# A planner's key that prefers settled operands, stores on ScalarE's queue, and another end of the last tile

## The chip, the core and the metric

The kernel runs on one core of one Trainium2 chip. The core has TensorE (PE in the profile), VectorE (DVE), ScalarE (ACT), GpSimd (POOL) and SyncE (SP); each executes its own list of instructions in a fixed order and waits at an instruction until what it depends on is done. SyncE only starts DMA transfers; ScalarE and GpSimd can start them too. The metric is the device time of one execution in microseconds; before and after the change it is the median of several executions.

## What is computed

One pre-norm residual block over x of 512 tokens by 1024 channels, in float32:

```
h = rmsnorm(x, norm_g)
q_lat, c_kv, k_rope, z_a, q_b, k_b, v_b, z_b, q_idx, k_idx, w_idx, gate_a, gate_b = split(h @ w_in)
y_a = mla_attention(...)  * silu(z_a)     # 8 heads, low-rank q and kv, rotary key, chunk-causal
y_b = dsa_attention(...)  * silu(z_b)     # 8 heads, an indexer keeps the top 128 keys of each query, relative-position bias
merged = sigmoid(gate_a) * (y_a @ w_o_a) + sigmoid(gate_b) * (y_b @ w_o_b)
out = rmsnorm(x + merged @ w_out, final_g)
```

## The kernel before

**Arithmetic.** Each float32 operand of a matmul is split in two parts, a rounded one (made by ScalarE, a copy at L302) and the rest (a subtraction by VectorE at L328 or GpSimd at L330), and each product is three matmuls (`mm3`, L405, issued at L400: high by high, high by low, low by high). So every weight tile goes through a load (SyncE, L427), a copy (ScalarE), a subtraction (VectorE or GpSimd) and only then the matmuls. Transposes are matmuls against an identity (L417). Scaling rows by a factor is VectorE at L358, GpSimd at L361 or ScalarE at L311; the power of -0.5 of a norm is GpSimd at L378; three-operand steps are VectorE at L339; reductions of scores are L1474 (branch A) and L1571 (branch B).

**Stages.** At the start x and the first weights come in; the indexer, key and latent projections run on unnormalised x, and the factor rstd of the first norm comes in later: four transposes (L417, tile rstd) bring it into a bank, ScalarE copies it to s_rbc, and VectorE uses s_rbc to make the normed input s_h. Then the gate, attention and latent projections follow as jobs in a written order, in which the matmuls of s_h by weight tiles fill TensorE while VectorE and ScalarE work on the heads of branch A (softmax, transposes of the probabilities s_p, products with values vv), then on the heads of branch B. A table of relative biases (bias_table, L835; two matmuls at L852) goes through a DRAM scratch. Eight gate tiles of branch A (w_ga, 128x512 each, tanh of the projection, tile s_sig) do not stay on chip: `gate` (L1170) stores each in that scratch, and `fetch_gates` (L1195) brings them back after the projections. Then both branches' output projections are merged, and the last product by w_out is made of seven block products (in the order 1, 7, 2, 6, 5, 4, 3) whose weight sums are made on chip by `out_job` (L1708 and following; the sums for products 6 and 4 come from the tiles of product 7).

**The order of the work.** The kernel's parts are Python generators that hand steps to a planner (`Flow`, L134 to L242). It holds a time for each engine, for the port that VectorE and GpSimd share and for the DMA, and costs for each step. In each round it takes, over all parts, the step with the smallest key (L204): the planned start, plus 0.01 times the part's priority, plus a small random nudge drawn from a seed (DRAW, L248). Where a step may run on several engines, it takes the one that ends soonest by the plan. The instruction is recorded at once, so the order of planning is the order of each engine's list on the chip. Nothing of the plan's times enters the program, only this order and the choice of engines. A step that is planned late moves all that comes behind it on its engine.

**The end.** The last product's results are read by `finish` (L1760): x is added, the squares are summed (by ScalarE in `square`, L1782, or for the last piece of a token tile by a VectorE reduce at L1768), and the row is multiplied by final_g. `scale_out` (L1786) adds the partial sums of squares with eps (L1790), adds the third one where a tile has three pieces (L1793), takes the power on GpSimd (L1795), scales the left half on VectorE and the right half on ScalarE (L1797), and has SyncE store both (L1800). The token tiles 2 and 3 end earlier, tiles 0 and 1 last.

Of the kernel before, what the change touches and what calls it, by code (L numbers as in the profile page):

```python
# [133 lines left out]
class Flow:  # L134
# [24 lines left out]
    def advance(self, t, value):  # L159
        try:  # L160
# [2 lines left out]
            t.alive = False  # L163
            self.threads.remove(t)

    def start(self, step, eng):
        s = self.free[eng]
        for b in step.ins:
            if not b.written and b not in step.outs:
                return math.inf  # L170
            s = max(s, b.w + (RAW_LAG.get(eng, 0.0) if b.by == eng else self.lat(b.by, eng)))
        for b in step.outs:
            if not eng == b.by == "SP":
                s = max(s, b.w + self.lat(b.by, eng))
            for e, r in b.reads.items():
                s = max(s, r + self.lat(e, eng))
        return max(s, self.port) if self.shares(step, eng) else s
# [5 lines left out]
    def run(self, stop=None):  # L183
        while self.threads:
            if stop and stop():
                return
            moved = False
            for t in sorted(self.threads, key=lambda t: t.prio):
                if isinstance(t.req, Get):
                    b = t.req.pool.give(t.req)  # L190
                    if b is not None:
                        self.advance(t, b)
                        moved = True
                elif isinstance(t.req, Until) and t.req.cond():
                    self.advance(t, None)
                    moved = True
            if moved:
                continue
            best = None
            for t in self.threads:  # L200
                if isinstance(t.req, Step):
                    for i, (eng, dur, emit) in enumerate(t.req.options):
                        s = self.start(t.req, eng)
                        key = (s + BIAS * t.prio + t.nudge, t.prio)  # L204
                        if len(t.req.options) > 1:
                            fin = s + dur + {"POOL": self.pbias if t.req.pbias is None else t.req.pbias, "ACT": t.req.abias}.get(eng, 0.0)
                            cand = (fin, s, eng, dur, emit, key)
                        else:
                            cand = (0.0, s, eng, dur, emit, key)
                        if i == 0 or cand[0] < mine[0]:  # L210
                            mine = cand
                    if best is None or mine[5] < best[1][5]:
                        best = (t, mine)
            if best is None or best[1][1] == math.inf:
                raise RuntimeError("stuck: " + "; ".join(f"{t.gen.__name__}@{t.gen.gi_frame.f_lineno} {type(t.req).__name__} {getattr(t.req, 'cls', '')}" for t in self.threads))
            t, (_, s, eng, dur, emit, _) = best
            emit()
            step = t.req
            if eng == "SP":

                self.free["SP"] = s + 0.05
                self.hw = max(self.hw, s) + (0.65 if step.ins and step.outs else 0.475)
                self.dma = max(self.dma, self.hw + 0.65)

                self.dma += dur * (SLOW if self.dma < 7.3 else 1.0)
                end = self.dma + (2.2 if step.ins and step.outs else 1.0) + step.late
            else:
                self.free[eng] = end = s + dur
                if self.shares(step, eng):
                    self.port = end  # L230
                if step.moves and eng == "ACT":

                    end += 1.8 + step.moves
                elif step.moves:
                    self.dma = max(self.dma, end + 1.0) + step.moves
                    end = self.dma + 1.0
            for b in step.ins:
                b.r = b.reads[eng] = max(b.r, end)
            for b in step.outs:
                b.w = max(b.w, end)  # L240
                b.written, b.by = True, eng
            self.advance(t, None)  # L242
# [2 lines left out]
RAW_LAG = {"DVE": 0.125, "POOL": 0.1, "ACT": 0.1}  # L245
BIAS = 0.01
NUDGE = 0.01
DRAW = 71  # L248
TC_ARGS = {}


# [1 line left out]
def tile_block(ctx: ExitStack, tc: tile.TileContext, a: dict, out: bass.AP, bias_dram: bass.AP):  # L253
# [181 lines left out]
    def act_dma(dst, src):  # L435
        step = Step([("ACT", 0.06, lambda: nc.scalar.dma_start(dst.ap, src))], bufs(dst), [])
        step.moves = 4.0 * dst.n * dst.ap.shape[0] / 360000
        return step

    def backward(v):  # L440
# [729 lines left out]
    def gate(name, c, how=proj):  # L1170


        def take(ps):
            if in_ps(ps.all):
                s = yield slot("sig")
                yield act(s.all.f, ps.all, AF.Tanh, scale=0.5)
                put(ps)
            else:
                s = ps
                yield act(s.all.f, s.all.f, AF.Tanh, scale=0.5)  # L1180
            if c in away and name == "w_ga":
                yield dma(spilt(c), s.all.f)
                put(s)
                done.add(("spilt", c))
            else:
                sig[name, c] = s

        how(name, c, take, 12)
# [3 lines left out]
    def spilt(c):  # L1192
        return bass.AP(bias_dram.tensor, NH * NREL + c * P * S, [[S, P], [1, S]])
# [514 lines left out]
    def out_job(product, c):  # L1708

        h, g = {1: (0, 0), 2: (0, 1), 3: (1, 1), 4: (0, 1), 6: (0, 0)}.get(product, (0, 0))  # L1710

        def prep(job):
            raw = [job.raw[:, 512 * i : 512 * i + 512] for i in range(2)]
            if product in (1, 2, 3):
                for i in range(2):
                    yield from split_b(raw[i], (product, 2 * c + i), i == 1)
            elif product in (5, 7):
                t = yield slot("wsum")
                yield soon(tt(t.all.f, raw[1], raw[0], ALU.subtract, BOTH))
                put(job.raw)  # L1720
                yield from split_b(t.all.f, (product, c), product == 5)
                if product == 7:
                    sums[c] = t
            else:
                for i in range(2):
                    yield Until(lambda: 2 * c + i in sums)
                    t = sums[2 * c + i].all.f
                    yield soon(tt(t, raw[i], t, ALU.add if product == 6 else ALU.subtract, BOTH))
                    if i == 1:
                        put(job.raw)  # L1730
                    yield from split_b(t, (product, 2 * c + i), product == 4)

        if product == 5:
            src = w_pair(w_block(0, 0, c), w_block(1, 0, c))
        elif product == 7:
            src = w_pair(w_block(1, 0, c), w_block(1, 1, c))
        else:
            src = a["w_out"][4 * h + 2 * g + c]
        Job(src, [512, 512], None, prep=prep)
# [20 lines left out]
    def finish(t, half, c0, c1, ps, nth, last, keep=False):  # L1760
# [4 lines left out]
            put(ps)  # L1765
        done.add(("read", t, nth))
        if last:
            step = Step([("DVE", 0.1 + 0.00104 * r.n, lambda: nc.vector.tensor_tensor_reduce(  # L1768
                junk.tile[:, : r.n], r.ap, r.ap, op0=ALU.mult, op1=ALU.add, scale=1.0, scalar=0.0,
                accum_out=ssf[t].tile[:, nth : nth + 1]))], [junk, ssf[t]], bufs(r))  # L1770
            step.count = 2
            yield step
            done.add(("sq", t, nth))
            yield is_done(("sum", t))
        else:
            spawn(square(t, r, nth), 0)
        if (t, half) not in rg:
            rg[t, half] = yield slot("rg")
        yield stt(rg[t, half].all.f[:, c0:c1], r, D ** 0.5, fg[half].all.f[:, c0:c1], ALU.mult, ALU.mult)
        done.add(("g", t, nth))  # L1780

    def square(t, r, nth):  # L1782
        yield act(junk[:, : r.n], r, AF.Square, accum=ssf[t][:, nth : nth + 1])
# [2 lines left out]
    def scale_out(t, count):  # L1786

        rs = yield Get(SMALL)
        yield Until(lambda: ("sq", t, 0) in done and ("sq", t, 1) in done)
        yield ts(rs[:, 0:1], ssf[t][:, 0:1], ssf[t][:, 1:2], D * EPS, ALU.add, ALU.add)  # L1790
        if count == 3:
            yield is_done(("sq", t, 2))
            yield tt(rs[:, 0:1], rs[:, 0:1], ssf[t][:, 2:3], ALU.add)  # L1793
        done.add(("sum", t))
        yield power(rs[:, 0:1])  # L1795
        yield Until(lambda: all(("g", t, i) in done for i in range(count)))
        for half, engs in ((0, ("DVE",)), (1, ("ACT",))):  # L1797
            x = rg[t, half].all.f
            yield scale_by(x, x, rs[:, 0:1], engs)
            yield dma(out[TOK[t], half * 512 : (half + 1) * 512], x)  # L1800

    def product(n, banks, left, cols, more=False):

# [256 lines left out]
```

## Time and profile before

| | |
|---|---|
| median of 3 runs | 426.47 us (426.45, 426.47, 428.28) |
| profiled execution, its own time | 427.16 us |
| its span in the trace | 425.4 us |
| granted clock of TensorE, mean | 0.995 |
| TensorE: matmul, weight loads | 415.3 us (98%), 363.9 us (86%) |
| VectorE, ScalarE, GpSimd | 380.5 us (89%), 262.2 us (62%), 109.5 us (26%) |
| matmuls | 2313 |
| DMA | 65.89 MB, mean 155 GB/s |

A row of a timeline reads: start and length in us, engine, line, operation, what it writes <- what it reads, shapes, and xN for N in a row of the same kind; in brackets the idle time of the engine in front of it and what released it. "SPq" and "ACTq" are the parts of SyncE and ScalarE that start transfers. Matmuls overlap (the next starts before the last has drained), so the length of one is more than its share, and the distance from start to start is the better measure. A row of the waits view gives: engine and line that waited, the engine, tile and line waited for, total us, times, longest.

### The profile page before, as it was taken

The numbers are of one execution on the slowest core, as the hardware profiler recorded it, in microseconds if no ns is written. First come the engines' busy times: TensorE is split into PE (matmuls) and PEld (weight loads), VectorE is DVE, ScalarE is ACT, GpSimd is POOL, SyncE is SP. The second block draws the span as 40 slices with busy tenths as digits, with TensorE's granted clock in tenths as the row PEclk, the third lists the DMA queues.
The fourth block names the chain that finished last, engine by engine and source line by source line (L and its number), as shares of the span: only waits on it lengthen the run. The fifth ranks groups of instructions, "written<-read, shape, count | busy, mean of one in ns | idle before, by whom it ended". The sixth has DMA issues, their size and how long they took to land.

```text
span 425.4 us, 7106 instructions
## 1 busy us (share of the span) xinstructions
PE 415.3 (98%) x2313; PEld 363.9 (86%) x2313; DVE 380.5 (89%) x815; ACT 262.2 (62%) x587; POOL 109.5 (26%) x131
## 2 busy tenths in 40 slices
PE   8999999999999999999999999999999999999993
PEld 6999868889888888888899988998998888888883
DVE  4789899999999999999879888988799757999995
ACT  6778786585573758544864677494598524436624
POOL 1037865455355723121300101000010002210212
PEclk9999999999999999999999999999999999999998
DMA  8973137817255450285243525425523887453705
GB/s 258 394 278 112 52 100 207 230 45 186 82 139 148 127 160 1 79 256 173 63 128 121 171 79 157 146 65 178 146 79 124 266 322 252 143 180 106 242 0 197
DMA packets 30277, 65.89 MB, mean 155 GB/s; under 512 B 4648, under 2 KB 5688, under 8 KB 30240
## 3 DMA queue, kind: packets, MB, share of 16 engines
q1 hardware_dynamic: 29264, 64.08, 48.5%
q0 software_dynamic: 832, 1.22, 0.9%
q8 instruction: 18, 0.29, 0.3%
q14 instruction: 19, 0.16, 0.1%
q10 hardware_dynamic: 144, 0.13, 0.1%
HBM read 50.49 MB, written 4.21 MB: 129 GB/s over the span
## 4 chain that ended last, share of the span: by engine, by line
PE 54%; DVE 30%; DMA 7%; ACT 4%; issue 4%; POOL 0%; POOLq 0%; SPq 0%; DVEq 0%; ACTq 0%
PE ps L400 50%; DVE mask L826 4%; DMA raw<-w_out 4%; DVE sm L825 3%; PE ps L417 2%; DVE sm L1474 2%; DVE s_ph L328 2%; DVE s_mg L328 2%; DVE s_wsum L328 1%; DMA s_sig<-bias_scratch 1%; DVE s_tmp L328 1%; ACT s_p L311 1%; DVE s_pair L328 1%; DVE s_wo L328 1%; DVE s_w L328 1%
## 5 line engine op out<-in xcount | busy, mean ns | idle before, releaser
L400 PE MATMUL ps<-s_h,s_w 128*128 128x512 f32 (+1 forms) x732 | 170.9, 379 | 0.0
L400 PEld LDWEIGHTS ps<-s_h,s_w 128*128 128x128 f32 x732 | 127.8, 189 | 21.8 <-issue 0.3
L302 ACT CAST s_w<-raw 128x512 fp32r<-128x512 f32 (+3 forms) x124 | 71.6, 593 | 17.8 <-DVE raw L328 9.2
L330 POOL TENSOR_TENSOR s_w<-raw,s_w 128x512 fp32r<-128x512 f32 (+2 forms) x35 | 44.7, 1284 | 130.1 <-ACT s_w L302 123.9
L328 DVE TENSOR_TENSOR s_w<-raw,s_w 128x512 fp32r<-128x512 f32 (+2 forms) x89 | 58.7, 670 | 5.3 <-ACT s_w L302 4.7
L400 PE MATMUL ps<-s_ys,s_w 128*128 128x512 f32 x192 | 43.7, 389 | 0.0
L400 PEld LDWEIGHTS ps<-s_ys,s_w 128*128 128x128 f32 x192 | 36.0, 188 | 7.5
L311 ACT ACTIVATE s_p<-s_p,sm 128x384 f32<-128x384 f32 (+3 forms) x54 | 29.2, 559 | 6.8 <-DVE sm L1571 5.6
L400 PE MATMUL ps<-s_wo,s_mg 128*128 128x512 f32 (+1 forms) x156 | 33.0, 373 | 0.0
L400 PE MATMUL ps<-s_w,s_xg 128*128 128x328 f32 (+1 forms) x192 | 32.5, 323 | 0.0
L400 PEld LDWEIGHTS ps<-s_wo,s_mg 128*128 128x128 f32 x156 | 27.6, 188 | 5.2
L400 PEld LDWEIGHTS ps<-s_w,s_xg 128*128 128x128 f32 x192 | 31.4, 188 | 0.0
L328 DVE TENSOR_TENSOR s_ph<-ps,s_ph 128x384 fp32r<-128x384 f32 (+1 forms) x48 | 27.4, 590 | 2.5 <-ACT s_ph L302 2.3
L302 ACT CAST s_ph<-ps 128x384 fp32r<-128x384 f32 (+1 forms) x48 | 23.5, 514 | 5.5 <-PE ps L417 4.2
L311 ACT ACTIVATE s_p<-ps,sm 128x128 f32<-128x128 f32 (+3 forms) x32 | 16.8, 527 | 15.5 <-DVE sm L1474 15.1
L826 DVE MATCH_REPLACE8 mask<-sm,mask 128x384 f32<-128x384 f32 (+2 forms) x48 | 25.8, 540 | 0.0
L825 DVE MAX8 sm<-mask 128x8 f32<-128x384 f32 (+2 forms) x48 | 25.5, 547 | 0.1
L400 PE MATMUL ps<-s_ph,vv 128*128 128x512 f32 (+3 forms) x128 | 24.9, 325 | 0.0
L417 PE MATMUL ps<-ident,s_p 128*128 128x128 f32 x160 | 24.2, 275 | 0.5 <-DVE s_p L358 0.3
L417 PEld LDWEIGHTS ps<-ident,s_p 128*128 128x128 f32 x160 | 18.8, 140 | 4.7 <-ACT s_p L311 1.0
L400 PEld LDWEIGHTS ps<-s_ph,vv 128*128 128x128 f32 x128 | 20.6, 189 | 2.1 <-DVE s_ph L328 0.2
L400 PE MATMUL ps<-s_lat,s_w 128*128 128x512 f32 x78 | 20.5, 398 | 0.0
(197 smaller groups left out, 737.5 us busy)
## 6 DMA issues: line engine op xcount, KB each, us to landing
raw<-w_out SPq DMA_DIRECT2D x18, 512.0 KB, 4.0
s_op<-s_op SPq DMA_DIRECT2D x36, 128.0 KB, 2.3
raw<-w_ga SPq DMA_DIRECT2D x8, 512.0 KB, 4.5
raw<-w_gb SPq DMA_DIRECT2D x8, 512.0 KB, 4.4
raw<-w_o SPq DMA_DIRECT2D x16, 256.0 KB
s_x<-xT SPq DMA_DIRECT2D x8, 256.0 KB, 4.9
s_xn<-x SPq DMA_DIRECT2D x8, 256.0 KB, 5.7
bias_scratch<-s_sig SPq DMA_DIRECT2D x8, 256.0 KB, 2.5
```

The lines of the kernel that those rows point to most:

```text
L302: nc.scalar.copy(dst.ap, src.ap)
L311: nc.scalar.activation(dst.ap, src.ap, func, **kw)
L328: opts.append(("DVE", 0.07 + 0.00104 * x.n, lambda: nc.vector.tensor_tensor(dst.ap, x.ap, y.ap, op=op)))
L330: opts.append(("POOL", 0.15 + 0.0021 * x.n, lambda: nc.gpsimd.tensor_tensor(dst.ap, x.ap, y.ap, op=op)))
L400: nc.tensor.matmul(ps.ap, l.ap, r.ap, start=start and i == 0, stop=stop and i == len(pairs) - 1, skip_group_check=more)
L417: nc.tensor.transpose(d.ap, s.ap, ident.tile)
L825: yield Step([("DVE", t, lambda: nc.vector.max(m8.tile, work.tile))], [m8], [work])
L826: yield Step([("DVE", t, lambda: nc.vector.match_replace(work.tile, m8.tile, work.tile, MARK))], [work], [m8])
L1474: yield Step([("DVE", 0.07 + 0.00104 * n, lambda: nc.vector.tensor_reduce(mx.tile[:, 1:2], ps.tile[:, :n], op=ALU.max, axis=AX.X, negate=T ...
```

## The change

Five things are edited.

1. `settled()` is added to the planner. For steps on PE and on SP the key uses, in place of the planned start, the latest of that start and, for each buffer read or written, the moment another engine last wrote or read it plus 2.0 us (PE, behind VectorE, ScalarE or GpSimd), 1.0 us (PE behind a transfer) or 1.0 us (SP behind one of the three). The start itself stays as planned; only the choice of the next step changes. The seed goes from 71 to 53.
2. The gates' stores are issued by ScalarE's queue (`act_move`).
3. The weight sums of product 4 wait in the plan until product 6's right operand exists.
4. In the tiles 0 and 1 the partial sum (eps and the two first pieces) is handed to the last reduce as its starting value, and the power reads its result; the separate add goes. Tile 0's left half is scaled by ScalarE. The last store (tile 1, right half) is issued by ScalarE's queue.
5. The part `square` gets the priority -50 in place of 0.

```
+    def settled(self, step, eng, start):
+        s = start
+        for b in (*step.ins, *step.outs):
+            for e, t in ((b.by, b.w), *b.reads.items()):
+                if e != eng and e in SETTLE[eng]:
+                    s = max(s, t + self.lat(e, eng) + SETTLE[eng][e])
+        return s
...
-                        key = (s + BIAS * t.prio + t.nudge, t.prio)
+                        key = ((self.settled(t.req, eng, s) if eng in SETTLE and s < math.inf else s) + BIAS * t.prio + t.nudge, t.prio)
...
-DRAW = 71
+DRAW = 53
+PSQUARE = -50
+SETTLE = {'PE': {'DVE': 2.0, 'ACT': 2.0, 'POOL': 2.0, 'SP': 1.0}, 'SP': {'DVE': 1.0, 'ACT': 1.0, 'POOL': 1.0}}
...
+    def act_move(dst, src):
+        d = dst.ap if isinstance(dst, View) else dst
+        step = Step([("ACT", 0.3, lambda: nc.scalar.dma_start(d, src.ap))], bufs(dst), bufs(src))
+        step.moves = 4.0 * src.n * src.ap.shape[0] / 360000
+        return step
...
             if c in away and name == "w_ga":
-                yield dma(spilt(c), s.all.f)
+                yield act_move(spilt(c), s.all.f)
...
-                    yield Until(lambda: 2 * c + i in sums)
+                    yield Until(lambda: 2 * c + i in sums and (product == 6 or (6, 2 * c + i) in right))
...
         if last:
+            yield Until(lambda: t in partial_sum)
+            s = partial_sum[t]
             step = Step([("DVE", 0.1 + 0.00104 * r.n, lambda: nc.vector.tensor_tensor_reduce(
-                junk.tile[:, : r.n], r.ap, r.ap, op0=ALU.mult, op1=ALU.add, scale=1.0, scalar=0.0,
-                accum_out=ssf[t].tile[:, nth : nth + 1]))], [junk, ssf[t]], bufs(r))
+                junk.tile[:, : r.n], r.ap, r.ap, op0=ALU.mult, op1=ALU.add, scale=1.0, scalar=s.tile[:, 0:1],
+                accum_out=s.tile[:, 1:2]))], [junk, s], [r.buf, s])
...
-            spawn(square(t, r, nth), 0)
+            spawn(square(t, r, nth), PSQUARE)
...
+        r = rs[:, 0:1]
         if count == 3:
-            yield is_done(("sq", t, 2))
-            yield tt(rs[:, 0:1], rs[:, 0:1], ssf[t][:, 2:3], ALU.add)
+            if t < 2:
+                partial_sum[t] = rs
+                yield is_done(("sq", t, 2))
+                r = rs[:, 1:2]
+            else:
+                yield is_done(("sq", t, 2))
+                yield tt(r, r, ssf[t][:, 2:3], ALU.add)
         done.add(("sum", t))
-        yield power(rs[:, 0:1])
+        yield power(r)
...
-        for half, engs in ((0, ("DVE",)), (1, ("ACT",))):
+        for half, engs in ((0, ("ACT",) if t == 0 else ("DVE",)), (1, ("ACT",))):
             x = rg[t, half].all.f
-            yield scale_by(x, x, rs[:, 0:1], engs)
-            yield dma(out[TOK[t], half * 512 : (half + 1) * 512], x)
+            yield scale_by(x, x, r, engs)
+            dst = out[TOK[t], half * 512 : (half + 1) * 512]
+            if t == 1 and half:
+                yield Step([("ACT", 0.06, lambda: nc.scalar.dma_start(dst, x.ap))], [], bufs(x))
+            else:
+                yield dma(dst, x)
```

More of the change, by code (lines that the diff above doesn't have):

```diff
@@ L1780, in finish @@
         done.add(("g", t, nth))
+    partial_sum = {}
     def square(t, r, nth):
```

## The prediction

> **What bounds the kernel now.** I read the page's head first: the span, and the busy time of each engine.
>
> ```profile
> span 425.4 us, 7106 instructions
> ...
> PE 415.3 (98%) x2313; PEld 363.9 (86%) x2313; DVE 380.5 (89%) x815; ACT 262.2 (62%) x587; POOL 109.5 (26%) x131
> ```
>
> TensorE (PE) is busy for 415.3 of 425.4 us, so 10.1 us of the span are not matmul. Both kernels hold the same 2313 matmuls, and the change takes none away. What it can win lies in those 10.1 us and in matmuls that start late although the row calls the engine busy. Next I cut the span by stages (columns: length, then busy time of PE, of its weight loads, of VectorE (DVE), ScalarE (ACT) and GpSimd (POOL), clock, DMA share, GB/s).
>
> ```profile
> 45.00:58.00 13.00, 12.03 (x68) 9.67 (x66) 11.06 (x17) 9.69 (x22) 10.86 (x15) 1.00 0.25 72
> 92.00:160.00 68.00, 68.00 (x374) 58.60 (x373) 67.66 (x172) 39.80 (x97) 35.05 (x42) 1.00 0.48 132
> 160.00:212.00 52.00, 51.74 (x258) 43.06 (x257) 49.94 (x109) 32.26 (x75) 13.64 (x12) 1.00 0.40 117
> 416.00:425.40 9.40, 2.57 (x22) 2.37 (x20) 4.98 (x15) 3.85 (x8) 1.69 (x3) 0.79 0.59 223
> ```
>
> Of the 10.1 us, 6.8 (9.40 less 2.57) lie in the end after the last matmul, and the stages between have tenths of a us to 1.0. In 92 to 160 PE has no gap at all, while VectorE works 67.66 of 68 us: there VectorE has no room, but its lateness does not yet reach PE. The view of PE's waits names what is left:
>
> ```profile
> PE ps L498 <- DVE neghalf L454: 1.1, 1, 1.1
> PE ps L852 <- DVE mask L339: 1.0, 1, 1.0
> ```
>
> The first is the start (L498, the warm-up) and stays: the two orders on PE agree for the first 166 instructions, to about 27 us. The second is one matmul at 57.97. The view counts only idle time; a matmul that is issued late also shows in the distance of starts. PE's timeline at three places (start, duration, of so many):
>
> ```profile
> 56.35 0.65 PE L803 MATMUL ps<-s_qs,s_qs 96*128 96x512 f32 x2
> 57.97 0.31 PE L852 MATMUL ps<-s_oh,rbs 64*8 64x320 f32 x1 [0.97 <-DVE mask L339]
> ```
> ```profile
> 165.04 0.94 PE L400 MATMUL ps<-s_h,s_w 128*128 128x512 f32 x3
> 165.82 0.49 PE L417 MATMUL ps<-ident,s_p 128*128 128x128 f32 x3
> 166.07 0.94 PE L400 MATMUL ps<-s_h,s_w 128*128 128x512 f32 x3
> 167.26 0.70 PE L417 MATMUL ps<-ident,s_p 128*128 128x128 f32 x3 [0.26 <-DVE s_p L358]
> ```
> ```profile
> 212.09 0.38 PE L417 MATMUL ps<-ident,s_p 128*128 128x128 f32 x2
> 212.73 0.44 PE L417 MATMUL ps<-ident,s_p 128*128 128x128 f32 x2 [0.25 <-ACT s_p L311]
> ```
>
> Three 128x512 matmuls take 0.78 us from start to start (165.04 to 165.82), 0.26 each; three transposes 0.25 (165.82 to 166.07), 0.083 each. So the matmul at 57.97 was due at 56.35 + 2 x 0.26 = 56.87 and is 1.10 late. That at 167.26 was due at 166.07 + 0.78 = 166.85: 0.41 late, and its group of three takes 0.70 in place of 0.49, 0.21 more. That at 212.73 was due at 212.09 + 2 x 0.083 = 212.26: 0.47 late. Together 2.2 us. This is all that I can find for a better order to win before the end.
>
> **The change part by part.** *The order (settled(), DRAW).* The key now favours, on PE, operands that were finished 2 us ago, so a matmul on a fresh operand is put behind others. I laid the two built orders side by side. Where a short chain of VectorE or ScalarE work springs from one matmul and another waits for its end, I added up the matmul work between them and took the chain's own durations off: less than 2 us is left over at 61 places before and at 12 after, less than 1 us at 14 and at 4. The late matmul at L852 now waits only for a ScalarE copy that starts 22 matmuls earlier. Number of waits: 434 before, 448 after, so waits are moved, not removed. I take the late time in proportion to the tight places: 2.2 x 12/61 = 0.4 stay, **-1.8 us**. Ends: all of it goes, -2.2; none goes, 0 (new waits could cost more: the slower rival).
>
> One place gets tighter. The four transposes of rstd come later:
>
> ```profile
> 25.70 1.20 PE L400 MATMUL ps<-s_xg,s_w 128*128 128x384 f32 x6
> 26.75 0.60 PE L400 MATMUL ps<-s_w,s_xg 128*128 128x328 f32 x3
> 27.19 0.60 PE L417 MATMUL ps<-ident,rstd 128*128 128x128 f32 x4
> ```
> ```profile
> 27.82 0.59 ACT L302 COPY s_rbc<-ps 128x512 f32<-128x512 f32 x1 [1.27 <-PE ps L417]
> ```
>
> Nine more 128x328 matmuls stand ahead of them (9 x 0.147 by 26.75 to 27.19: VectorE's work on the normed input starts up to 1.3 us later), and behind them only three 128x384 matmuls before one that writes the bank that the copy at 27.82 must first have read; before, twelve stood there. From the last transpose's start, 27.19 + 3 x 0.083 = 27.44, to the copy's end at 28.41 are 0.97 us. The last transpose and three matmuls at 0.175 (25.70 to 26.75 for six) cover 0.61: **+0.3 us** (0.36, less an unknown bit since ScalarE may be free sooner). Ends 0 and 0.4, plus 1.3 if VectorE's lateness reached a matmul; I take it as covered, since the next late matmul is 30 us on.
>
> *VectorE and GpSimd.* The planner's choices shift: VectorE 764 to 746 instructions in the built order, ScalarE 503 to 519 (9 of these issue stores), GpSimd 134 to 144. VectorE's relief I cost at nothing: in the stage where it has no room, PE has no gap to give back. GpSimd's extra is a rival's.
>
> *The gates' stores.* Eight 256 KB stores go from SyncE's queue to ScalarE's.
>
> ```profile
> SPq L427 <- ACT s_sig L311: 11.9, 4, 7.5
> ```
> ```profile
> 55.26 0.33 SPq L427 DMA_DIRECT2D bias_scratch<-s_sig  x1
> ```
> ```profile
> 0.73 0.41 ACTq L436 DMA_DIRECT2D s_er<-w_qi  x1
> ```
>
> SyncE's queue stood 11.9 us behind such stores, with weight loads behind them; now these go sooner. ScalarE has just made s_sig itself, so it waits for nobody there and pays the issue: 8 x 0.41 = 3.3 us, against 62% busy. No wait of PE names a DMA, so the loads gain nothing: 0. Ends: -0.5 (loads that let a weight split start sooner) and +3.3 (every issue delays a copy that PE awaits; the nearest row, ScalarE's 39.80 of 68, speaks against it). The Trainium skill, "DMA: Bandwidth & Descriptors", section "Issuing engines are not separate DMA queues", says that starting DMAs from several engines saves only the sequencer's time for starting them, usually small beside the transfer. By it the move is worth 8 x 0.33 = 2.6 us of SyncE, which would change my sum by nothing; the waits row differs, since SyncE was held 11.9 us by stores that were not ready.
>
> *The sums of weights for product 4* wait for product 6's operand: an order on VectorE beside a PE that is 100% busy; 0, ends -0.2 and +0.5 (one VectorE operation late at PE).
>
> *The end.* The tail's rows:
>
> ```profile
> 419.16 0.72 ACT L311 ACTIVATE s_rg<-s_rg,sm 128x512 f32<-128x512 f32 x1 [0.30 <-POOL sm L378]
> 419.36 0.48 DVE L358 TENSOR_SCALAR s_rg<-s_rg,sm 128x512 f32<-128x512 f32 x1
> 419.75 0.42 DVE L1768 CUSTOM_DVE_ANT_0 junk<-s_xr 128x256 f32<-128x256 f32 x1
> 419.86 2.61 SPq L427 DMA_DIRECT2D out<-s_rg  x4
> 420.09 0.08 DVE L1768 DVE_READ_ACCUMULATOR2_ANT ssf<- 128x1 f32 x1
> 420.21 0.16 DVE L328 TENSOR_TENSOR sm<-sm,ssf 128x1 f32<-128x1 f32 x1
> 420.29 0.42 DVE L339 SCALAR_TENSOR_TENSOR s_rg<-s_xr,s_fg 128x256 f32<-128x256 f32 x1
> 420.45 0.66 POOL L378 TENSOR_TENSOR sm<-sm,neghalf 128x1 f32<-128x1 f32 x1 [1.32 <-DVE sm L328]
> 421.15 0.72 ACT L311 ACTIVATE s_rg<-s_rg,sm 128x512 f32<-128x512 f32 x1 [1.27 <-POOL sm L378]
> ```
>
> The scale at 419.36 moves to ScalarE, so the reduce starts at 419.36 and not 419.75 (-0.39); the separate add goes, and GpSimd's power starts 0.2 sooner after the read at 420.09 (0.28 less some 0.08 to hand over). Power begins at about 419.86 and ends at 420.5. But ScalarE now scales three halves: 419.16 + 2 x 0.72 = 420.6, only then the last: 420.6 in place of 421.15, **-0.5**. Its store is issued by ScalarE right behind (421.35 to 421.75), where SyncE's four stores ended at 419.86 + 2.61 = 422.47: up to -0.7. I take -0.5, ends -0.2 (the issue waits for the engine to drain) and -0.7.
>
> **Sum:** -1.8 + 0.3 - 0.5 = -2.0 us. The profiled execution took 427.16 us (span 425.4 and 1.76 around it), so 425.2; it is 0.69 above the median of the runs, 426.47, so on the median **424.5**.
>
> **Rivals.** (a) *The order changes nothing, only the end does*: each wait that goes is replaced by one of the same size (434 waits against 448 speak for it; the counts of tight places against): 426.47 - 0.5 = 426.0. (b) *All gains at their ends*: -2.2 - 0.5 - 0.7 = -3.4, 423.1; for it, the L852 stall alone is half. (c) *GpSimd slows VectorE in front of PE, and it is slower.* The late matmul at 167.26 comes from this:
>
> ```profile
> 165.57 0.96 DVE L358 TENSOR_SCALAR s_p<-s_p,sm 128x512 f32<-128x512 f32 x1
> ```
> ```profile
> 165.14 1.11 POOL L330 TENSOR_TENSOR s_tmp<-s_tmp 128x256 f32<-128x256 f32 x1 [6.08 <-DVE sm L1441]
> ```
>
> The same scale took 0.48 at 419.36, with GpSimd idle; here it took 0.96 beside a GpSimd operation. Ten more GpSimd operations come, and in 92 to 160 VectorE has 0.34 us of room. Price: up to 1.1 us for a stall like that at 57.97. Five of them turn -2.0 into +3.5, 430.0; to be slower than 428.6 it takes four. The filler matmuls left behind the last head of branch A shrink from 60 to 30 (7.8 us at 0.26), which speaks for it; that VectorE loses 18 operations speaks against. The Trainium skill, "GPSIMD Engine Reference", section "1. Specifications", has GpSimd share its SBUF interfaces with VectorE, with contention where VectorE reads two inputs from SBUF or runs in a two-port mode. The rows at 165.57 and 165.14 agree; no run here shows which mode it was. (d) *The change doesn't do what it says*: the late time stays because hardware times differ from the planned ones; it gives (a)'s time.
>
> **How the numbers follow.** About 0.5% (2.1 us: below 424.34 or above 428.60) is what a measurement of this kernel can tell from no change. The forecast case, 423.8 to 425.3, gets 0.45 and straddles 424.34; (b) and near it 0.20; (a) and (d), 425.3 to 427.0, 0.20; (c) 0.15, most of it beyond 428.6. The first gives 0.23 to faster and 0.22 to the same; (b) adds 0.20 to faster; (a) and (d) 0.20 to the same, and (c) 0.02 to the same and 0.13 to slower. Faster 0.43, same 0.44, slower 0.13. The range goes from 423.0 ((b), and the small gains of loads) to 427.3 ((a) with the bank stall and one new late matmul: 426.0 + 0.3 + 1.0).
>
> **What would show it.** Right: no wait of PE at L852 and L417 over 0.2 us, stages 45 to 58 and 160 to 212 with PE fully busy, one gap of 0.3 us near 28.5, the last power starting about 0.5 us behind the reduce's start (0.7 now), the last store issued by ACTq. Wrong: PE waits of over 1 us in sum behind 92 us, above all for L358 or L328 of VectorE with a GpSimd row beside them; a wait of PE for a DMA; ScalarE's copies late behind an ACTq row; or a span whose loss lies in the first 27 us, where I expect no difference.

## The result and the profile after

| | before | changed |
|---|---|---|
| runs beside each other, 20 each: median (lowest to highest) | 428.25 us (426.27 to 429.81) | 425.64 us (425.31 to 427.45) |
| ratio of the two, 95% interval | | 0.9954 (0.9938 to 0.997) |
| profiled execution, span | 427.16, 425.4 us | 425.62, 423.8 us |

The ratio goes by the means of the runs. The change makes the kernel faster by 0.46% (0.30 to 0.62%), 2.0 us on 426.47. The two profiled executions differ by 1.54 us, the two lowest runs by 0.96. In the profiles of three kernels below (the order alone, the additions late, the seed 12) the matmuls at about 7 us run slower, which costs some 1.6 us (last section); how many of the timed runs began so is not known, so I compare profiles by places behind 10 us.

The page of the changed kernel, its head:

```profile
span 423.8 us, 7086 instructions
...
PE 414.7 (98%) x2313; PEld 364.3 (86%) x2313; DVE 368.9 (87%) x797; ACT 265.1 (63%) x594; POOL 132.3 (31%) x141
```

VectorE is busy 11.6 us less, GpSimd 22.8 us more, TensorE as before. The stages that the prediction showed, and two more (same columns):

```profile
45.00:58.00 13.00, 13.00 (x71) 10.77 (x70) 10.01 (x16) 10.56 (x23) 11.49 (x14) 1.00 0.33 99
58.00:92.00 34.00, 34.00 (x172) 29.05 (x172) 23.98 (x47) 23.30 (x57) 18.26 (x19) 1.00 0.57 160
92.00:160.00 68.00, 68.00 (x376) 58.83 (x375) 65.91 (x178) 42.15 (x102) 36.68 (x45) 1.00 0.48 132
160.00:212.00 52.00, 52.00 (x270) 44.43 (x269) 51.60 (x116) 31.15 (x70) 24.30 (x25) 1.00 0.41 120
212.00:260.00 48.00, 47.19 (x334) 43.90 (x334) 42.40 (x90) 32.56 (x73) 2.75 (x2) 1.00 0.38 124
415.00:423.80 8.80, 2.43 (x21) 2.23 (x19) 4.06 (x12) 4.40 (x9) 1.33 (x2) 0.84 0.63 238
```

TensorE has no gap left from 45 to 58 (0.97 us before) and from 160 to 212 (0.26). But from 212 to 260 it now idles 0.81 us; the same row of before shows 0.25:

```profile
212.00:260.00 48.00, 47.75 (x353) 45.15 (x352) 40.58 (x84) 31.56 (x68) 1.36 (x1) 1.00 0.40 125
```

TensorE's waits after the change. The wait at the bias table and those at the transposes are gone; two waits for steps on s_pair (0.6 us for VectorE, 0.2 for ScalarE) and one for the copy s_rbc are new:

```profile
PE ps L516 <- DVE neghalf L472: 1.1, 1, 1.1
PE ps L411 <- DVE s_pair L339: 0.6, 1, 0.6
PE ps L411 <- ACT s_xg L322: 0.5, 1, 0.5
PE ps L411 <- DVE s_xg L350: 0.2, 1, 0.2
PE ps L411 <- ACT s_pair L313: 0.2, 1, 0.2
PE ps L411 <- ACT s_rbc L313: 0.2, 1, 0.2
```

The bank of the rstd copy, in the changed kernel's PE timeline:

```profile
25.49 1.20 PE L411 MATMUL ps<-s_xg,s_w 128*128 128x384 f32 x6
...
28.31 0.60 PE L428 MATMUL ps<-ident,rstd 128*128 128x128 f32 x4
28.67 0.77 PE L411 MATMUL ps<-s_w,s_xg 128*128 128x384 f32 x3
29.59 0.62 PE L411 MATMUL ps<-s_w,s_xg 128*128 128x384 f32 x2 [0.16 <-ACT s_rbc L313]
```

Three 128x384 matmuls last 0.52 us from start to start; the next began 0.92 behind the first, so 0.40 late: the new stall that the prediction named. The six matmuls at 25.49 stood at 25.70 before: 0.21 us of lead comes from the start, where the order is the same.

Where TensorE stands ahead can be read from groups that both kernels have. First the group of 48 matmuls, and what follows; before:

```profile
220.19 5.92 PE L400 MATMUL ps<-s_w,s_hs 128*128 128x256 f32 x48
225.95 3.04 PE L400 MATMUL ps<-s_w,s_h 128*128 128x256 f32 x24
```

and after:

```profile
217.86 5.92 PE L411 MATMUL ps<-s_w,s_hs 128*128 128x256 f32 x48
223.62 3.04 PE L411 MATMUL ps<-s_w,s_h 128*128 128x256 f32 x24
227.23 2.03 PE L411 MATMUL ps<-s_w,s_hs 128*128 128x256 f32 x15 [0.57 <-DVE s_pair L339]
```

At the 48 matmuls, and at the 24 behind them, the changed kernel is 2.33 us ahead; then a matmul waits. The last product's 36 matmuls show what is left; before, then after:

```profile
412.77 5.80 PE L400 MATMUL ps<-s_wo,qhi 128*128 128x512 f32 x36
```
```profile
411.63 5.80 PE L411 MATMUL ps<-s_wo,qhi 128*128 128x512 f32 x36
```

1.14 us ahead: half of the gain was given back between 223 and 412. The end behind this point (span less 412.77 and 411.63) takes 12.6 us before and 12.2 after.

What gives it back? VectorE's row at the wait, and SyncE's loads, in the changed kernel:

```profile
225.79 0.69 DVE L339 TENSOR_TENSOR s_wsum<-raw 128x512 f32<-128x512 f32 x1 [0.91 <-DMA raw<-w_gb]
226.40 0.68 DVE L339 TENSOR_TENSOR s_pair<-ps,s_pair 128x512 f32<-128x512 f32 x1
```
```profile
219.28 2.17 SPq L438 DMA_DIRECT2D raw<-w_gb  x2
```

and in the kernel before:

```profile
225.38 0.68 DVE L328 TENSOR_TENSOR s_wsum<-raw 128x512 f32<-128x512 f32 x1
...
226.70 0.68 DVE L328 TENSOR_TENSOR s_pair<-ps,s_pair 128x512 f32<-128x512 f32 x1
```
```profile
219.43 1.58 SPq L427 DMA_DIRECT2D raw<-w_gb  x2
```

The step on s_wsum needs the second of the two loads of w_gb, and the read of the bank (s_pair) stands behind it in VectorE's list. Both loads wait for a raw buffer that a VectorE step frees. The first starts at 219.28 (219.43 before), and the issue of the second ends at 221.45 (219.28 + 2.17) where it ended at 221.01 (219.43 + 1.58) before. So VectorE, busy 51.60 of the 52 us up to 212, had gained nothing: the read of the bank starts at 226.40 in place of 226.70, 0.3 us earlier, while TensorE came 2.33 earlier. At 0.12 us for a matmul (48 in 5.76, 220.19 to 225.95) the 24 at 223.62 are through by 226.50, so the next, at 227.23, is 0.73 late. A second matmul is 0.39 late, behind a copy by ScalarE (231.62 + 12 x 0.12 = 233.06 was due):

```profile
231.62 1.60 PE L411 MATMUL ps<-s_hs,s_w 128*128 128x256 f32 x12
233.45 1.70 PE L411 MATMUL ps<-s_h,s_w 128*128 128x256 f32 x12 [0.23 <-ACT s_pair L313]
```

These two places make up the 1.2 us. In short, TensorE ran 2.3 us ahead of a supply that had hardly moved, and met it. This is read from one trace of each kernel; no run below changes these waits alone.

### The profile page after: what moved, and what is told of

The parts are those of the page before. It is cut to its first block, busy times and chain, and to the rows that moved or that the text cites. A ratio compares the mean times of both kernels' runs of the same rounds, so it can differ in the third digit from the quotient of the medians.

```text
span 423.8 us, 7086 instructions
## 1 busy us (share of the span) xinstructions
PE 414.7 (98%) x2313; PEld 364.3 (86%) x2313; DVE 368.9 (87%) x797; ACT 265.1 (63%) x594; POOL 132.3 (31%) x141
## 4 chain that ended last, share of the span: by engine, by line
PE 91%; DVE 3%; DMA 2%; ACT 2%; issue 1%; POOL 0%; POOLq 0%; DVEq 0%; ACTq 0%; SPq 0%
PE ps L411 81%; PE ps L428 5%; PE ps L1510 1%; PE ps L1511 1%; PE ps L1509 1%; DMA raw<-w_gb 1%; PE ps L821 1%; DVE s_w L339 1%; DMA s_er<-w_qi 1%; ACT s_w L313 1%; DVE raw L339 1%; DVE s_xr L350 1%; POOL sm L389 0%; DVE s_pair L339 0%; ACT s_p L322 0%
## 5 line engine op out<-in xcount | busy, mean ns | idle before, releaser
L341 POOL TENSOR_TENSOR s_w<-raw,s_w 128x512 fp32r<-128x512 f32 (+2 forms) x43 | 55.4, 1296 | 56.2 <-ACT s_w L313 39.0
L339 DVE TENSOR_TENSOR s_w<-raw,s_w 128x512 fp32r<-128x512 f32 (+2 forms) x81 | 52.5, 664 | 3.5 <-ACT s_w L313 3.0
L322 ACT ACTIVATE s_p<-s_p,sm 128x128 f32<-128x128 f32 (+3 forms) x60 | 31.2, 550 | 5.3 <-DVE sm L1589 4.9
L341 POOL TENSOR_TENSOR s_pair<-s_pair 128x256 f32<-128x256 f32 x2 | 2.2, 1108 | 99.1 <-DVE s_pair L339 97.8
L844 DVE MATCH_REPLACE8 mask<-sm,mask 128x256 f32<-128x256 f32 (+2 forms) x48 | 25.8, 541 | 0.0
L843 DVE MAX8 sm<-mask 128x8 f32<-128x256 f32 (+2 forms) x48 | 25.4, 548 | 0.3
L313 ACT COPY s_tmp<-ps 64x512 f32<-64x512 f32 (+1 forms) x18 | 10.1, 563 | 19.2 <-PE ps L411 19.2
```

The lines of the kernel that those rows point to most:

```text
L313: nc.scalar.copy(dst.ap, src.ap)
L322: nc.scalar.activation(dst.ap, src.ap, func, **kw)
L339: opts.append(("DVE", 0.07 + 0.00104 * x.n, lambda: nc.vector.tensor_tensor(dst.ap, x.ap, y.ap, op=op)))
L341: opts.append(("POOL", 0.15 + 0.0021 * x.n, lambda: nc.gpsimd.tensor_tensor(dst.ap, x.ap, y.ap, op=op)))
L843: yield Step([("DVE", t, lambda: nc.vector.max(m8.tile, work.tile))], [m8], [work])
L844: yield Step([("DVE", t, lambda: nc.vector.match_replace(work.tile, m8.tile, work.tile, MARK))], [work], [m8])
```

## The experiments

All ratios are to the kernel before, on the same chip. The waits and stages are from the profile of each run.

**The end alone.** The edits of the end put into the kernel before; TensorE's built order is that of before. Diff: points 4 and 5 of the change.

> The kernel before with the end's edits alone (partial sum into the last reduce, tile 0's left half on ScalarE, last store by ScalarE's queue, priority of the squares); TensorE's built order is that of before, instruction by instruction. My theory (order and end both pay): the last power starts about 0.5 us behind the reduce's start, the end after the last matmul's start is 0.4 us shorter (7.10 before, 6.70 in the changed kernel), and the time falls by 0.3 to 0.5 us, ratio near 0.999. Rival (the order changes nothing, only the end does): the whole difference of the changed kernel, ratio near 0.9954. TensorE's late waits stay: 1.1 us at the second matmul of the bias table, 0.4 and 0.5 at the transposes.

Measured: 0.9993 (0.997 to 1.0015). The wait at the bias table stays. In its profile the last power starts 0.57 us behind the reduce's start (419.46 and 418.89), and the end behind the start of the last 36 matmuls takes 12.0 us (412.42 of 424.4) in place of 12.6. In the time the end by itself is worth too little for this measurement, as expected of a few tenths.

**The order alone.** Diff to before: point 1 of the change (`settled()`, SETTLE, `DRAW = 53`).

> The kernel before with the planner's settled key and the seed 53 alone; gates' stores on SyncE's queue, the end as before. My theory: TensorE's late time falls by about 1.1 to 1.8 us (the three late matmuls go, the stall of 0.3 us at the bank of the rstd copy comes), ratio 0.996 to 0.9975. Rival (only the end pays): ratio 1.000 within 0.001.

Measured: 0.9959 (0.9938 to 0.998). So the order carries the change; the rival that only the end pays falls. In its profile the six 128x384 matmuls that start at 25.70 before start at 27.06, 1.36 later, and the last 36 matmuls at 413.06, only 0.29 later: between these two places the order won 1.07 us. In the changed kernel it won 0.93 between them (0.21 ahead, then 1.14).

**The gates' stores back on SyncE.**

```
-                yield act_move(spilt(c), s.all.f)
+                yield dma(spilt(c), s.all.f)
```

> The changed kernel with the gates' eight stores back on SyncE's queue; 70 of TensorE's 2328 instructions stand elsewhere. My theory (the stores' queue is worth nothing): within 0.3 us of the changed kernel. Rival (SyncE held up by stores that are not ready makes weight loads late): 1 us or more slower than the changed kernel, with waits of TensorE behind weight splits; a second rival (ScalarE's eight issues of 0.34 to 0.41 us are on the path): 0.5 us or more faster.

Measured: 0.9956 (0.9938 to 0.9974), profiled execution 425.56 us (changed kernel: 425.62). The store queue is worth nothing that shows, in either direction. Point 3 of the change and the squares' priority leave the built order as it is, instruction by instruction, when each is taken out, so they have no effect here.

**The last store back on SyncE.**

```
-            if t == 1 and half:
+            if False:
```

> The changed kernel with the very last store back on SyncE's queue; all other instructions are the same. In the changed kernel ScalarE's issue at 419.98 lands at 422.745, 2.76 us later, where SyncE's last store of before took 2.26. Theory A (ScalarE's queue starts a transfer later than SyncE's): by SyncE the store is issued at 420.12 and lands at 422.3 to 422.4, the time falls by 0.3 to 0.4 us. Theory B (the landing is set by three stores of 256 KB that come within 0.8 us of each other): it lands at 422.75 to 422.9, the time is the same or 0.15 us longer.

Measured: 0.9945 (0.9921 to 0.9968), profiled execution 425.60 us. The time from issue to landing of the stores of `out` (least, median, greatest of the three whose landing the trace has), in the changed kernel and here:

```profile
DMA to landing us min/median/max: 2.0/2.3/2.8
```
```profile
DMA to landing us min/median/max: 2.0/2.3/2.6
```

SyncE issues 0.23 us later (420.22 in place of 419.98) and its store takes 2.6 in place of 2.8 us: it lands at the same time, about 422.8. That fits theory B, that three stores of 256 KB close to each other set the landing and not the queue.

**The seed alone, and the key alone.** Before with `DRAW = 53`; before with `settled()` and SETTLE at seed 71.

> The kernel before with the seed 53 in place of 71 and nothing else: its built order has 29 places with less than 1 us and 62 with less than 2 us of matmul work in hand (before: 14 and 61). Theory A (the settled key makes the gain, the seed is chance): late time of TensorE as in before or above, 2 us and more behind 27 us, time 0 to 2 us above before. Theory B (the seed was the gain): time 0.7 to 2 us below before.

> The kernel before with the settled key at the old seed 71: 5 places under 1 us and 12 under 2 us, as few as in the changed kernel (4 and 12). Theory A (the key makes the gain): TensorE's late time falls below 1.5 us, no wait at the bias table, time near that of the order alone with seed 53 (0.7 to 2 us below before). Theory B (the seed): time within 0.5 us of before.

Measured: seed alone 1.0242 (1.0205 to 1.028), key alone 1.0218 (1.0179 to 1.0257). Both theories of both runs fall: neither part makes the gain, each alone costs 9 to 10 us. TensorE's late time on short chains did fall with the key alone (no wait at the bias table), but it meets this, in the last stage:

```profile
408.44 6.02 POOL L340 TENSOR_TENSOR s_wo<-s_wsum,s_wo 128x512 fp32r<-128x512 f32 x1
...
409.64 3.68 DVE L338 TENSOR_TENSOR s_xr<-s_xr,s_part 128x512 f32<-128x512 f32 x6
...
415.79 0.67 DVE L338 TENSOR_TENSOR s_wo<-s_wsum,s_wo 128x512 fp32r<-128x512 f32 x1
416.52 0.74 PE L410 MATMUL ps<-s_wo,s_mg 128*128 128x512 f32 x2 [3.65 <-DVE s_wo L338]
```

VectorE's list has six additions of s_xr, and more work for the end, in front of the weight split that the next matmuls need. With the seed alone the same wait is 6.5 us. The built orders show it before any run: a split of s_wo behind the additions in these two and in the next kernel, none in the kernel before and the changed one. A planner that takes what can start first puts the additions in as soon as they are ready; which side the split falls on then differs from order to order.

**A wider margin.** SETTLE for TensorE 4.0 in place of 2.0.

> The changed kernel with 4.0 us in place of 2.0 us on TensorE: 3 places under 1 us, none under 0.5 (changed kernel: 4 and 1), 15 under 2 us, and no tight place at the bank of the rstd copy. My theory (late time goes with the tight places): the 0.3 us stall at 29.6 is gone, late time at or below the changed kernel's, time 0.3 us less. Rival (behind 92 us VectorE sets the pace, and a wait taken away at one place comes back at the next): the early stall goes, but waits of TensorE between 200 and 260 us grow by as much, time the same within 0.2 us; third (a wider margin puts off work on the chains of the heads): slower by 0.5 us or more.

Measured: 1.0226 (1.0173 to 1.0278). The stall at the rstd copy is gone, as the counts said, but TensorE waits 4.5 us for a split of s_wo, 2.3 for s_pair and 1.2 for s_w: the counts of short chains say nothing of these.

**VectorE prefers landed loads too.** `'DVE': {'SP': 1.0}` added to SETTLE.

> The changed kernel with one more entry: on VectorE an operand that a transfer brought less than 1.0 us ago counts as late too. In the changed kernel VectorE stands 0.9 us at 225.79 for a load of w_gb, with a step behind it for which TensorE then waits 0.6 us at 227.23. My theory: that wait goes, the stage from 212 to 260 loses 0.5 to 0.8 us of idle time, time 0.5 us below the changed kernel. Rival (VectorE is behind anyhow, being busy 51.6 of 52 us before): TensorE waits as long, but for another step of VectorE; time the same within 0.3 us.

Measured: 1.0072 (1.005 to 1.0094). The wait for s_pair is gone, but TensorE waits 1.3 us for two splits of s_w, 0.6 for s_p and 0.6 for a transfer of s_qs. Its built order has a split of s_wo behind the additions too, but for a later matmul, and no wait came of it. Nothing was won; the order changed everywhere, so this doesn't isolate that wait.

**The additions late.** The key alone at seed 71, and

```
-            spawn(partial(i), 0)
+            spawn(partial(i), 40)
```

> The kernel with the settled key at seed 71 alone, whose TensorE stood 3.7 us for the last weight split of product 5 or 4 (tile s_wo) because VectorE had six additions of s_xr in front of it; here the part that makes these additions has the priority 40 in place of 0, which in the built order puts no split behind all of them. Theory A (that order is the stall): the wait on s_wo goes, the time falls by 3.5 to 4.5 us, to 432 to 433; what stays above before is the stage from 212 to 260 (4 us of idle time of TensorE). Theory B (GpSimd, held up by VectorE's additions from 408.4 to 414.5, is the stall): TensorE still waits, on a split that GpSimd makes, 2 us or more.

Measured: 1.0135 (1.0103 to 1.0167), against 1.0218 with the additions early: 3.5 us less. No wait for s_wo is left. Theory A: the place of the six additions was the stall. Of the 5.8 us that remain above before, 3.6 are waits in the stage from 212 to 260, 2.4 for s_w and 1.2 for a sum, as in the kernel with the key alone.

**TensorE's part of the key alone.** `'SP'` taken out of SETTLE, from the changed kernel.

> The changed kernel without the key's part for SyncE (TensorE's part stays at 2.0 us). In the four kernels with the whole key VectorE is busy only 8 to 10 of 17 us from 75 to 92, since the top-128 search starts at 97 to 104 us and not at 81 as before; in the built orders the last score matmul of the first tile stands at 87 us of matmul work with SyncE's part of the key, at 75 without it. Theory A (VectorE's lost 8 us come back as waits of TensorE behind 212 us): the search starts at 79 to 84, VectorE is busy 15 us or more from 75 to 92, TensorE's lost time from 212 to 260 is below the changed kernel's 2.6 us, and the time is 0.5 to 1 us below the changed kernel's. Theory B (VectorE's idle time there costs nothing, the waits behind 212 come from the loads of w_gb): the stage from 212 to 260 as in the changed kernel, time within 0.3 us of it or above.

Measured: 0.9968 (0.9949 to 0.9986). By these intervals it can't be told from the changed kernel, though in its profile the last 36 matmuls start at 413.95, 2.3 us later than in the changed one: TensorE waits 0.6 in place of 0.2 us at the rstd copy and 0.8 for two steps on s_op before 92 us, which the changed kernel does not. VectorE's stretch from 75 to 92, before, changed, and here:

```profile
75.00:92.00 17.00, 16.81 (x47) 1.00 0.61 169
```
```profile
75.00:92.00 17.00, 8.13 (x18) 1.00 0.55 157
```
```profile
75.00:92.00 17.00, 16.91 (x82) 14.33 (x83) 15.72 (x42) 9.85 (x28) 5.45 (x6) 1.00 0.58 174
212.00:260.00 48.00, 46.71 (x338) 44.03 (x338) 40.11 (x85) 29.24 (x64) 3.14 (x2) 1.00 0.46 136
```

(In the last, VectorE is the third figure of busy time.) So SyncE's part of the key does take 8.7 us of work from VectorE there: the top-128 search starts at 102 us in the changed kernel, at 80.9 before and at 83.5 here. But giving it back does not stop the waits behind 212: 1.29 us of idle time here, with VectorE standing 1.9 us for a load of w_gb. Theory A's last step falls; this run speaks for the loads (theory B), without changing them alone.

**The scores exempt as well.** The 24 score matmuls planned by the old key, from the run before.

> As the one before, and the 24 score matmuls are exempt from the key, so two tiles' scores end at 77 us of matmul work. Theory A: the search starts by 84, VectorE is busy from 75 to 92 as before the change, time at or below the kernel with TensorE's part alone. Theory B: no difference from it within 0.5 us. A third outcome, a new wait of TensorE at the scores (built order: two places without any matmul work in hand), would show as L821 or L870 in TensorE's waits and cost up to 1 us.

Measured: 0.9998 (0.9977 to 1.0018). The search starts at 86 us and the time is not below that of the run before, so theory A falls. TensorE has no gap at all from 212 to 260. It reaches the group of 48 matmuls there at 221.19, 1.0 us later than the kernel before, so it brings no lead that it could lose. The third outcome came, dearer than the 1 us expected at most: 1.64 us of wait at the scores:

```profile
51.49 3.23 DVE L341 TENSOR_TENSOR s_tmp<-s_tmp,ropes 32x512 f32<-32x512 f32 x1
```
```profile
51.62 2.54 POOL L343 TENSOR_TENSOR s_w<-raw,s_w 128x512 fp32r<-128x512 f32 x2
```
```profile
55.81 0.44 PE L823 MATMUL ps<-s_qs,s_qs 96*128 96x384 f32 x1 [1.64 <-DVE mask L360]
```

A VectorE product of 32x512 takes 3.23 us beside two GpSimd operations (a step of the same kind and size at 55.79 in this run: 0.68), and the mask that TensorE waits for stands behind it. That is the prediction's rival (c), with its mechanism and a price of 1.6 us, in another order than the one predicted.

**Twenty-five seeds, the best by counts.** TensorE's part alone with `DRAW = 12`.

> TensorE's part of the key alone (as in the kernel with TensorE's part alone) with the seed 12, picked out of 25 seeds by counts of the built order alone: no weight split behind the six additions of s_xr (so in 13 of the 25), the scores of two tiles done at 76 us of matmul work (87 to 92 in the changed kernel), 11 places under 2 us (changed kernel: 12), 3 under 0.5 us (changed kernel: 1). Theory (these three counts are what the order's time hangs on): no wait on s_wo in the last stage, the top-128 search before 84 us, less lost by TensorE from 212 to 260 us than in the changed kernel, and a time within 0.8 us of the changed kernel's or below it. Rival (the counts leave out what decides, such as VectorE's own queue and the landing of loads): a time 1 us or more above the changed kernel's, from a wait that none of the three counts names.

Measured: 1.0191 (1.0153 to 1.0229). The rival holds: the counts leave out what decides. No split of VectorE stood behind the additions, but one of GpSimd did:

```profile
413.79 5.26 POOL L341 TENSOR_TENSOR s_wo<-s_wsum,s_wo 128x512 fp32r<-128x512 f32 x1 [0.73 <-ACT s_wo L313]
414.22 3.70 DVE L339 TENSOR_TENSOR s_xr<-s_xr,s_part 128x512 f32<-128x512 f32 x6
...
419.11 1.28 PE L411 MATMUL ps<-s_wo,s_mg 128*128 128x512 f32 x4 [3.67 <-POOL s_wo L341]
```

GpSimd's subtraction, 1.30 us at 406.36 in this run, lasts 5.26 while VectorE runs the additions, and TensorE waits 3.67 us for it. Five splits of s_w cost it another 3.2 us.

No version beats the changed kernel by more than the intervals.

## Why the prediction was right, and where it was not

- **The late matmuls (-1.8).** Right in place: the waits at the bias table and at the transposes are gone, and by 218 us the changed kernel was 2.33 ahead. Less the 0.21 of the start, plus the 0.40 paid at the rstd copy, the order had won 2.5 by then, somewhat more than the 2.2 that I could find. It was wrong in what stays: by the last product 1.14 is left, so the order with its rstd stall is worth 0.9 (1.07 in the run of the order alone) and not 1.5. The step that failed is "I take the late time in proportion to the tight places: 2.2 x 12/61 = 0.4 stay": 1.2 us came back behind 223, at places that the count does not know, most of it at a VectorE step on a load in front of the read that TensorE needed. The prediction had the fact (VectorE busy 67.66 of 68) and drew from it only that VectorE's relief is worth nothing, not that TensorE's lead is worth nothing once it meets VectorE's supply.
- **The rstd bank (+0.3).** Right: 0.40 by the starts. Its view shows only 0.16 of idle time; the distance of starts tells it.
- **VectorE and GpSimd at nothing.** The relief of VectorE showed nothing in the time, as forecast, but no run isolates it. What the term left out is VectorE's supply: most of the 1.2 us that came back behind 223 were lost to it. The form was not foreseen either: SyncE's part of the key left VectorE idle for 8.7 us more from 75 to 92, and giving that work back won nothing. Of GpSimd's 22.8 us of added busy time some 8.8 are no added work: two weight splits of 128x512 took 11.45 us, where one took 1.30 in the run with the seed 12, beside VectorE's steps of that time, the six additions among them. TensorE did not wait for them here:

```profile
398.19 11.45 POOL L341 TENSOR_TENSOR s_wo<-raw,s_wo 128x512 fp32r<-128x512 f32 x2
```
- **The gates' stores at nothing, product 4 at nothing.** Right: shown by the run with the stores on SyncE, and for product 4 by built orders that don't differ. The rule of the Trainium skill, "DMA: Bandwidth & Descriptors", section "Issuing engines are not separate DMA queues", and the waits row differ in what the move might be worth; in the time neither showed.
- **The end (-0.5).** Nearly right: 0.4 by the profiles (12.6 to 12.2), too little to show in the time of the run with the end alone. Rows of the changed kernel:

```profile
417.96 0.48 DVE L1788 CUSTOM_DVE_ANT_0 junk<-s_xr,sm 128x256 f32<-128x256 f32 x1
418.37 0.08 DVE L1788 DVE_READ_ACCUMULATOR2_ANT sm<- 128x1 f32 x1
418.37 0.42 DVE L350 SCALAR_TENSOR_TENSOR s_rg<-s_xr,s_fg 128x256 f32<-128x256 f32 x1
418.53 0.66 POOL L389 TENSOR_TENSOR sm<-sm,neghalf 128x1 f32<-128x1 f32 x1 [0.93 <-DVE sm L1788]
```

  The power starts 0.57 behind the reduce's start (0.70 before; 0.5 was forecast). The store by ScalarE's queue gains nothing: from SyncE's queue it landed at the same time.
- **The rivals.** (a) falls with the order alone (0.9959). (c) did not show in the changed kernel's waits. It happened in one order beside it (the scores exempt), and with the seed 12 in the other direction: VectorE held up GpSimd, and TensorE waited for GpSimd. (d) falls too: the late matmuls that it would keep are gone.
- **The sum.** -2.0 forecast, -2.0 by the ratio, -1.54 by the two profiles. That the ratio meets the forecast is in part luck. By the places above the change won 0.9 by the order and 0.4 by the end, and 0.2 of the profiles' 1.54 stem from the start, where the order is the same. What makes the other 0.7 of the ratio's 2.0 stays open; the order alone shows nearly the same ratio.
- **What it missed altogether**: that the key pays only with some seeds. Four of the neighbouring orders cost about 2%, and the longest single wait in each, 3.7 to 6.5 of some 8 to 10 us, is for one weight split behind or beside the six additions. The counts of short chains, on which the forecast of the order stood, were about as low as the changed kernel's for three of them: the key alone, the wider margin and the seed 12.

## What to carry to other kernels

Where a planner writes the order, a new rule in its key is not an edit with an effect of its own: each variant is another draw, so read the built order for the few places that cost much (a step that feeds the busiest engine behind a run of steps that feed nothing yet) and measure the finished order, not the rule. A gain on the busiest engine can be lost where it meets the supply of the next busiest, as it seems to have been here; look for the same group of instructions in both traces and follow the lead from place to place. Put work that only the end needs behind every split that the busiest engine still waits for: here that was worth 3.5 us.

## What the runs showed of the hardware

- VectorE and GpSimd hold each other up. A GpSimd subtraction of 128x512 took 1.30 us (seed 12, at 406.36) while VectorE, from 406.41 on, ran steps with one input in a bank; it took 5.26 and 6.02 beside additions of VectorE with both inputs in SBUF (rows above). A VectorE product of 32x512 took 0.68 with GpSimd idle and 3.23 beside GpSimd. The Trainium skill, "GPSIMD Engine Reference", section "1. Specifications", names the shared SBUF interfaces and VectorE instructions with two SBUF inputs; these rows agree, and they show that the loser can be held up for a whole run of the other's instructions (413.79 to 419.05 around the six additions from 414.22 to 417.92).
- The same matmuls of the first 10 us can take 1.6 times as long in another execution. In the profile of the order alone, and then in that of the changed kernel:

```profile
7.15 3.12 PE L410 MATMUL ps<-s_w,s_xg 128*128 128x328 f32 x12
```
```profile
6.75 1.95 PE L411 MATMUL ps<-s_w,s_xg 128*128 128x328 f32 x12
```

  3.12 against 1.95 us for the same twelve, while the granted clock reads 1.00 in both (5 to 10 us):

```profile
5.00:10.00 5.00, 5.00 (x20) 4.98 (x21) 3.75 (x8) 3.77 (x10) 0.00 (x0) 1.00 1.00 347
```
```profile
5.00:10.00 5.00, 4.76 (x29) 4.44 (x30) 3.70 (x7) 3.43 (x8) 0.00 (x0) 1.00 0.99 332
```

  The Trainium skill, "TensorE: Matmul & The Clock Gate", section "🔬 Part 1: The HAM clock gate (the "warmup" mystery)", says that the first microseconds of matmuls run at half the clock and that how many do differs from run to run; the rows differ between two executions in this way, but by 1.6 and not by 2, and the clock column shows no such state: that this is the cause is not shown.
- A store of 256 KB landed 2.0 us after its issue at the least; as the third of three issued within 0.8 to 1.0 us it took 2.8 from ScalarE's queue and 2.6 from SyncE's.
